# A fifth raw weight buffer, fewer early conditioning products and a later gate in a two-layer decoder trunk

## The chip, the cores and the metric

The kernel runs on one core of one Trainium2 chip. The metric is the device time of one execution in microseconds (us). The core has TensorE for matrix products (PE in the profile, its weight loads PEld), VectorE (DVE), ScalarE (ACT), GpSimd (POOL) and SyncE (SP), whose queue starts nearly all DMA transfers here. Lower is better.

## The reference

Two layers of a decoder trunk, 256 tokens by 1024 features, in float32. Each layer has three sublayers: a SwiGLU feed-forward block (FFN), a token mixer, and a second FFN. Layer 0 mixes tokens with an HGRN2 gated linear recurrence, layer 1 with a chunked gMLP. Around each sublayer stand an RMSNorm before and after, and a shift, scale and gate that come from the conditioning vector c:

```python
cond = silu(c)
mod = (cond @ ada_w[i] + ada_b[i])            # 9 vectors of 1024 per layer
h = rms_norm(x, pre_g) * (1.0 + scale) + shift
x = x + res_w * gate * rms_norm(fn(h), post_g)
# fn of an FFN: (silu(h @ w_a) * (h @ w_b)) @ w_out
# fn of HGRN2, per head, with b the running sum of log f in chunks of 64 tokens:
#   log_f = logaddexp(log lb, log1p(-lb) + log_sigmoid(fx));  k = (1 - lb) * sigmoid(-fx)
#   o = (q exp(b)) @ state + sum over s <= t of q_t exp(b_t - b_s) k_s v_s
#   state = state * exp(b_last) + sum of k exp(b_last - b) v
#   out = (rms_norm(o) * silu(g)) @ w_out
```

## The kernel before

**Products.** TensorE multiplies in a form with rounded operands (fp32r). To keep the accuracy of float32, every weight and every activation is split into a high and a low part, and each product is three: high by high, high by low, low by high (`mm3`, L162; `mm3f`, L462; `out_mm`, L416). So every weight tile is loaded in two halves of 128x1024 into a buffer of the pool `raw`, rounded by ScalarE into the high tile (`cast`, L113, the copy at L122) and subtracted by VectorE to give the low tile (`sub`, L129, at L132). High and low tiles come from the pool `whl` of 14. `raw` has 4 buffers: a load into one can start when the subtraction that read it last is done. All loads stand in SP's queue in program order (`load`, L56), so a load that waits for its buffer holds those behind it.

**Conditioning products.** The shift, scale and gate vectors are 144 products of VectorE (`ada`, L181, the product at L194), each over a 128x1024 tile of 512 KB that has to be loaded first. `pace` (L156) spreads them over the weight blocks: `pace(upto, blocks)` sets a rate, and `wblock` (L141) does so many products for each block prepared, up to a limit. The norm before the second sublayer needs the first 40 of them, that before the third needs 64. In the first sublayer the limit is 50 (`bgs["ffn0"]`), spread over 23 blocks; the boundary to the second adds two; in the HGRN sublayer the limit is 64, spread over 9 blocks.

**The order of work.** Between sublayers and in their first units (`open`, L303, to `close`, L392) the order on TensorE, VectorE and ScalarE is the written one. Elsewhere a scheduler places instructions at compile time by program order, readiness and buffers, but `after` (L59) holds one instruction behind another on its engine. `self.gate` holds a product behind another product, `self.hold` holds casts, subtractions and conditioning products behind given ones, and `table` (L72) places ScalarE's function tables between their users.

**The head** (`start`, L1107, and `first_h`, L1167). c is spread to all partitions by a product (L1125), `cond` is its silu. The sums of squares of x (L1133) give r; the two 128x1024 tiles of x are scaled by r, the first half of the features on VectorE (L1143), the second on ScalarE (L1145), transposed by TensorE (L1149) and copied by ScalarE into `xnT` (L1150), 16 transposes and 4 copies in all. Between the square root and the rest the silu table is loaded. The first products (L578) go by blocks of 128 features, `kc` 0 to 7: for each block `first_h` makes two conditioning products, from these the columns `A` and `sh` (L1173, L1174), then `hf = A * xnT + sh` on ScalarE (L1177), its rounding to the high part on ScalarE (L1179) and the low part on VectorE (L1180); 48 products follow, sorted in the first seven blocks by part. They gather in eight PSUM banks, four of which are those that held the transposes.

**The HGRN sublayer** (`hgrn`, L648). The eight heads are worked in two halves of four. For each half `feat` (L656) makes the projections of f and q in pairs of heads (`pr` 0 and 1); `gate_f` (L689) turns f's projection into k, b (the running sum) and nk: its first part (L694 to L698) reads the projection in PSUM, its second (L701 to L714) makes log f, the running sum (a scan, L710) and k. It works in a tile `L`, which for `pr` 1 is the only tile of the pool `lp`. `attn` (L716) computes the scores of a half in seven levels of halving block size: for each level `prep` (L720) makes an operand X with two subtractions and a multiplication on VectorE (L727, L732, L737) around an exponential on ScalarE, sixteen (or eight) small products follow (L755), and a masked copy (L768). `zip_steps` (L873) interleaves the levels of `attn(0)` with the projections, the gate and the values of the second half (L914 to L917), one step of the latter per level, after a lead of five; and `attn(1)` with the norm and output products of the first half (L956). `norm` (L926) scales eight 128x128 blocks of the first half's heads by their inverse norm on ScalarE (L828, called at L941); TensorE transposes them (L837), ScalarE and VectorE split them (L845, L846), and the first output products (L164) follow.

Of the kernel before, what the change touches and what calls it, by code (L numbers as in the profile page):

```python
# [10 lines left out]
F32 = mybir.dt.float32  # L11
# [4 lines left out]
ALU = mybir.AluOpType  # L16
# [17 lines left out]
class Body:  # L34
    def __init__(self, ctx, tc, ins, out):
# [4 lines left out]
        self.raw = pool("raw", 4)  # L40
# [3 lines left out]
        self.lp = pool("lp", 1)  # L44
# [444 lines left out]
    def ffn(self, f, hT, G_fn, pre_next, nxt, bg):  # L489
# [76 lines left out]
        if f == 0:  # L566
# [3 lines left out]
            for kc in range(KC):  # L570
                self.first_h(kc)
                wb = nb()
# [17 lines left out]
        if f == 0:  # L590
            self.pace(bg, 23)
        for u in range(len(pend), 11):
# [17 lines left out]
            if u == 8:  # L610
                G = G_fn()
        pre_next()
# [35 lines left out]
    def hgrn(self, hT, G_fn, pre_next, nxt, bg):  # L648
        nc, tc = self.nc, self.tc
        self.pace(bg, 9)  # L650
# [38 lines left out]
        def gate_f(hb, pr, z):  # L689

            L = self.lp.tile([P, 512], F32, tag="L", name="L") if pr else self.scr.tile([P, 512], F32, tag="hf", name="L")
# [9 lines left out]
            for h, sl in hs:  # L701
                nc.scalar.activation(L[:, sl], b[:, sl], AF.Abs, bias=col(self.ldiff, h))
            for h, sl in hs:
                nc.scalar.activation(b[:, sl], b[:, sl], AF.Relu, bias=col(self.ldiff, h))
            self.act_exp(L, L, scale=-1.0)
            self.tact(L, L, AF.Ln, bias=1.0)
            for h, sl in hs:
                nc.vector.scalar_tensor_tensor(b[:, sl], b[:, sl], col(self.loglb, h), L[:, sl],
                                               op0=ALU.add, op1=ALU.add)
                nc.vector.tensor_tensor_scan(b[:, sl], self.rmask, b[:, sl], 0.0, ALU.mult, ALU.add)  # L710
            for h, sl in hs:
                self.act_exp(k[:, sl], nk[:, sl], scale=-1.0, bias=col(self.log1mlb, h))
                nc.vector.scalar_tensor_tensor(nk[:, sl], nk[:, sl], col(self.log1mlb, h), b[:, sl],
                                               op0=ALU.subtract, op1=ALU.add)  # L714

        def attn(hb, bank, res):  # L716
# [3 lines left out]
            def prep(h):  # L720
# [7 lines left out]
                if h == 64:  # L728
                    self.act_exp(Xv[:, :, 0, :], Xv[:, :, 0, :])
                    self.act_exp(Xv[:, :, 1, :], bv[:, :, 1, :])  # L730
                else:
                    nc.vector.tensor_sub(Xv[:, :, 1, :], bv[:, :, 1, :], ref)  # L732
                    if h == 1:
                        self.act_exp(Xv[:, :, 1, :], Xv[:, :, 1, :])
                    else:
                        self.act_exp(X, X)
                return X, nc.vector.tensor_mul(Xv[:, :, 1, :], Xv[:, :, 1, :], qv[:, :, 1, :])  # L737
# [135 lines left out]
        def zip_steps(a, b, lead):  # L873

            b = list(b)
            def step():
                while b:
                    if next(b[0], a) is not a:
                        break
                    b.pop(0)  # L880
# [6 lines left out]
            self.gate = None  # L887
            run(*b)

        pg = self.res  # L890
# [35 lines left out]
        def norm():  # L926
# [13 lines left out]
            for u in range(2):  # L940
                scale(state["norm"][u], r[:, 4 * u:4 * u + 4], True)  # L941
# [165 lines left out]
    def start(self):  # L1107
# [4 lines left out]
        row = self.scr.tile([1, D + P], F32, tag="xn", name="row")  # L1112
        self.load(row[:, 0:D], self.d["c"])
# [7 lines left out]
        nc.vector.memset(row[:, D:], 1.0)  # L1121
        for h in range(2):
            hs = slice(512 * h, 512 * h + 512)
            ps = self.acc.tile([P, 512], F32, tag="acc", name="cps")
            nc.tensor.matmul(ps, row[:, D:], row[:, hs], start=True, stop=True)  # L1125
# [12 lines left out]
        self.table("silu_and_others")  # L1138
        for h in range(2):
            hs = slice(512 * h, 512 * h + 512)  # L1140
            for t in range(NT):
                if h == 0:
                    nc.vector.tensor_scalar(xn[t][:, hs], self.x[t][:, hs], r[:, t:t + 1], None, op0=ALU.mult)  # L1143
                else:
                    nc.scalar.activation(xn[t][:, hs], self.x[t][:, hs], AF.Copy, scale=r[:, t:t + 1])  # L1145
                ps = self.yps.tile([P, 512], F32, tag=f"y{t}{h}", name="xps")
                for k in range(4):
                    kc = 4 * h + k
                    nc.tensor.transpose(ps[:, k * P:(k + 1) * P], xn[t][:, kc * P:(kc + 1) * P], self.ident)  # L1149
                nc.scalar.copy(self.xnT[:, 4 * h:4 * h + 4, t * P:(t + 1) * P],  # L1150
                               ps.rearrange("p (k t) -> p k t", k=4))
# [15 lines left out]
    def first_h(self, kc):  # L1167

        nc = self.nc
        self.ada(2 * kc + 2)  # L1170
        A, sh = self.c0
# [155 lines left out]
```

## Time and profile before

Three runs took 1161.33, 1159.75 and 1160.45 us, median 1160.45. The numbers of the profile come from one more execution.

| | |
|---|---|
| profiled execution, device time | 1161.51 us |
| its span, first to last instruction | 1159.7 us |
| TensorE clock granted, mean | 0.995 |
| bytes moved by DMA | 282.31 MB, 243 GB/s in the mean |
| conditioning products, VectorE | 144, 174.8 us |
| weight subtractions (L132), VectorE | 376, 452.5 us |
| weight casts (L122), ScalarE | 376, 387.1 us |

How to read the profile: a row of a timeline gives start and duration in us, engine, line, operation, the tiles written and read, shapes and a count of merged instructions; in square brackets stands how long the engine was idle before it and what it waited for. A row of waits gives total, number and longest. A row with two times and a colon is a stretch of the span, with its length, the busy time of PE, PEld, DVE, ACT and POOL, the granted clock, the DMA share and GB/s. Spans of products overlap, since they are pipelined, so an engine's busy time is the union of its spans. Durations of a merged row are their union too.

### The profile page before, as it was taken

How to read it: one execution, taken by the hardware profiler on the slowest of the kernel's cores; microseconds unless marked ns; L12 is line 12 of the kernel's file. 1: busy time of each engine (PE TensorE's matmuls, PEld its weight loads, DVE VectorE, ACT ScalarE, POOL GpSimd, SP SyncE). 2: the span in 40 equal slices, each digit the busy share in tenths (PEclk: the TensorE clock that was granted, in tenths of full speed). 3: DMA queues.
4: the chain of work that ended last, by engine and by line, in shares of the span. 5: the costliest groups of instructions: out<-in, count | busy, mean ns of one | idle time of the engine just before them, and what ended most of it. 6: DMA issues, size and time to landing. Idle time of an engine off the chain costs nothing.

```text
span 1159.7 us, 17073 instructions
## 1 busy us (share of the span) xinstructions
PE 1133.2 (98%) x6518; PEld 987.8 (85%) x6518; DVE 897.7 (77%) x1359; ACT 672.0 (58%) x1065; POOL 6.8 (1%) x16
## 2 busy tenths in 40 slices
PE   7999999999999999999999999999999999999997
PEld 6999997799887888888888888888999888888886
DVE  6997877998797898875699986666987876775832
ACT  5453445887786764555765555644764457654631
POOL 0000000000000000000000000000000000000000
PEclk9999999999899999999999999999999999999999
DMA  9999998585434599986299987427787763875720
GB/s 345 324 329 333 330 339 317 201 305 180 145 103 147 198 351 330 341 284 202 65 356 343 331 304 252 146 84 260 258 294 259 275 219 98 266 245 195 246 100 37
DMA packets 79764, 282.31 MB, mean 243 GB/s; under 512 B 9873, under 2 KB 10561, under 8 KB 79682
## 3 DMA queue, kind: packets, MB, share of 16 engines
q1 hardware_dynamic: 78626, 278.05, 68.6%
q0 software_dynamic: 1056, 3.17, 0.7%
q8 instruction: 51, 0.84, 0.3%
q14 instruction: 31, 0.25, 0.1%
HBM read 280.11 MB, written 1.07 MB: 242 GB/s over the span
## 4 chain that ended last, share of the span: by engine, by line
PE 83%; DVE 8%; DMA 5%; ACT 2%; issue 2%; DVEq 0%; SPq 0%; ACTq 0%
PE ups L458 17%; PE ups L459 9%; PE y L164 8%; PE y L166 8%; PE y L165 8%; PE pps L433 6%; PE ups L578 4%; PE ups L464 4%; PE ups L466 4%; PE ups L465 4%; DVE w L132 3%; DMA ada<-in_ada 2%; DMA raw<-in_wffn 2%; PE ab L755 1%; DMA raw<-in_whg 1%
## 5 line engine op out<-in xcount | busy, mean ns | idle before, releaser
L132 DVE TENSOR_TENSOR w<-raw,w 128x1024 fp32r<-128x1024 f32 x376 | 452.5, 1221 | 86.0 <-ACT w L122 85.0
L122 ACT CAST w<-raw 128x1024 fp32r<-128x1024 f32 x376 | 387.1, 1049 | 150.9 <-DMA raw<-in_wffn 71.2
L458 PE MATMUL ups<-h,w 128*128 128x512 f32 x864 | 302.4, 393 | 0.1
L459 PE MATMUL ups<-h,w 128*128 128x256 f32 x864 | 242.1, 280 | 0.0
L194 DVE CUSTOM_DVE_ANT_0 ada<-ada,cond 128x1024 f32<-128x1024 f32 x144 | 174.8, 1219 | 25.9 <-DMA ada<-in_ada 25.9
L458 PEld LDWEIGHTS ups<-h,w 128*128 128x128 f32 x864 | 161.8, 187 | 37.0 <-PE ups L459 0.4
L164 PE MATMUL y<-w,t 128*128 128x512 f32 x448 | 178.1, 399 | 0.9 <-ACT t L169 0.9
L165 PE MATMUL y<-w,t 128*128 128x512 f32 x448 | 177.2, 396 | 1.4 <-DVE w L132 1.4
L166 PE MATMUL y<-w,t 128*128 128x512 f32 x448 | 176.9, 396 | 0.4 <-DVE t L170 0.4
L459 PEld LDWEIGHTS ups<-h,w 128*128 128x128 f32 x864 | 163.3, 189 | 1.0
L464 PE MATMUL ups<-h,w 128*128 128x256 f32 x416 | 118.4, 285 | 0.0
L466 PE MATMUL ups<-h,w 128*128 128x256 f32 x416 | 117.7, 283 | 0.0
L465 PE MATMUL ups<-h,w 128*128 128x256 f32 x416 | 117.6, 283 | 0.0
L433 PE MATMUL pps<-w,h 128*128 128x512 f32 x480 | 113.9, 393 | 0.7 <-DVE h L293 0.7
L433 PEld LDWEIGHTS pps<-w,h 128*128 128x128 f32 x480 | 89.0, 188 | 19.4 <-DVE h L293 1.2
L166 PEld LDWEIGHTS y<-w,t 128*128 128x128 f32 x448 | 84.2, 188 | 21.1 <-DVE t L170 1.0
L164 PEld LDWEIGHTS y<-w,t 128*128 128x128 f32 x448 | 84.3, 188 | 20.6 <-ACT t L169 1.5
L165 PEld LDWEIGHTS y<-w,t 128*128 128x128 f32 x448 | 84.3, 188 | 20.6 <-DVE w L132 2.7
L464 PEld LDWEIGHTS ups<-h,w 128*128 128x128 f32 x416 | 79.7, 192 | 1.1 <-issue 0.2
L465 PEld LDWEIGHTS ups<-h,w 128*128 128x128 f32 x416 | 79.7, 192 | 0.8 <-issue 0.2
L466 PEld LDWEIGHTS ups<-h,w 128*128 128x128 f32 x416 | 79.7, 192 | 0.0
L80 ACT ACTIVATE t<-t 128x256 f32<-128x256 f32 (+2 forms) x70 | 36.2, 522 | 39.0 <-DVE t L511 37.5
(202 smaller groups left out, 1303.7 us busy)
## 6 DMA issues: line engine op xcount, KB each, us to landing
raw<-in_wffn SPq DMA_DIRECT2D x264, 512.0 KB, 5.6
ada<-in_ada SPq DMA_DIRECT2D x144, 512.0 KB, 6.7
raw<-in_wgmu SPq DMA_DIRECT2D x48, 512.0 KB, 5.6
raw<-in_whg SPq DMA_DIRECT2D x40, 512.0 KB, 5.6
raw<-in_wgmv SPq DMA_DIRECT2D x24, 512.0 KB, 4.8
G<-gflat POOLq DMA_DIRECT2D x6, 512.0 KB, 6.5
t<-in_gbin SPq DMA_DIRECT2D x6, 256.0 KB, 5.9
x<-in_x SPq DMA_DIRECT2D x2, 512.0 KB, 4.2
```

The costliest lines, as they stand in the source:

```text
L122: self.after(self.nc.scalar.copy(hi[:, sl], raw), self.hold[0])
L132: self.after(self.nc.vector.tensor_sub(lo[:, sl], raw, hi[:, sl]), self.hold[1])
L164: self.paced(mm(ps, l[0], r[0], start=start, stop=False))
L165: mm(ps, l[0], r[1], start=False, stop=False)
L166: mm(ps, l[1], r[0], start=False, stop=stop)
L194: self.after(nc.vector.tensor_tensor_reduce(t, t, self.cond, 1.0, 0.0, ALU.mult, ALU.add, self.mod[i // 24][:, i % 24:i % 24 + 1]), self.h ...
L433: lambda g=g, i=i, j=j, kc=kc, w=w: mm(res[g][t], h2[:, i, t, kc, :], w, start=kc + i + j == 0, stop=i == 1 and kc == KC - 1)))
L458: self.paced(mm(ps, u[0], self.h2[:, :, :, kc, :], start=kc == 0, stop=False))
L459: self.last = mm(ps[:, 1, :], u[1], self.h2[:, 0, :, kc, :], start=False, stop=kc == KC - 1)
L464: self.paced(mm(o, u[0], h[0], start=start, stop=False))
L465: mm(o, u[0], h[1], start=False, stop=False)
L466: self.last = mm(o, u[1], h[0], start=False, stop=stop)
```

## The change

- **Buffers.** `raw` has five buffers. The pool `lp` is gone; the second pair's `L` in `gate_f` comes from the pool `p2` (`t2`), which has four. The row of ones for the first product moves into a tile of its own.
- **Head.** The scalings of both halves of x come first. Then only the first half of the features is transposed and copied (`turn(0)`). `first_h(0)` issues the first half weight cast ahead of its hf, rounds h with VectorE in place of ScalarE, and makes the first half weight subtraction and the other transposes and copies behind that, the copies ordered after hf. All later conditioning products and subtractions stay behind the first low part (`self.hold`). The silu table is loaded at the third block.
- **Conditioning products.** In the first sublayer up to 36 over 19 blocks, and from the ninth unit on up to 44 over 10. In the HGRN sublayer up to 64 over 11 blocks in place of 9. The total is unchanged.
- **Gate.** For the second half of the heads `gate_f` makes only its first part at once; the second (`rest`) is put into `later` and issued two steps on. Its first ScalarE operation is ordered behind the latest level's exponential, its first VectorE operation behind that level's multiplication.
- **Norm.** Of the eight scalings in `norm` the last four go to VectorE (L830's form) in place of ScalarE.

The diff, cut to its core:

```diff
-        self.raw = pool("raw", 4)
+        self.raw = pool("raw", 5)
-        self.lp = pool("lp", 1)
@@ ffn
                 self.first_h(kc)
-                wb = nb()
+                if kc == 2:
+                    self.table("silu_and_others")
+                if kc == 0:
+                    self.halves(1)
+                    wb = self.ready.pop(0)
+                else:
+                    wb = nb()
...
-            self.pace(bg, 23)
+            self.pace(36, 19)
...
                 G = G_fn()
+                if f == 0:
+                    self.pace(bg, 10)
@@ hgrn
-        self.pace(bg, 9)
+        self.pace(bg, 11)
...
-            L = self.lp.tile([P, 512], F32, tag="L", name="L") if pr else self.scr.tile([P, 512], F32, tag="hf", name="L")
+            L = self.t2() if pr else self.scr.tile([P, 512], F32, tag="hf", name="L")
...
+            def rest():
+                e, last = state.get("level", (None, None))
+                for h, sl in hs:
+                    self.after(nc.scalar.activation(L[:, sl], b[:, sl], AF.Abs, bias=col(self.ldiff, h)), e)
...
+                for h, sl in hs:
+                    self.after(nc.vector.scalar_tensor_tensor(b[:, sl], b[:, sl], col(self.loglb, h), L[:, sl],
+                                                              op0=ALU.add, op1=ALU.add), last)
+                    nc.vector.tensor_tensor_scan(b[:, sl], self.rmask, b[:, sl], 0.0, ALU.mult, ALU.add)
...
+            if hb:
+                later.extend([None, True, rest])
+            else:
+                rest()
@@ prep
-                return X, nc.vector.tensor_mul(Xv[:, :, 1, :], Xv[:, :, 1, :], qv[:, :, 1, :])
+                last = nc.vector.tensor_mul(Xv[:, :, 1, :], Xv[:, :, 1, :], qv[:, :, 1, :])
+                state["level"] = e, last
+                return X, last
@@ zip_steps
             def step():
+                if later and later.pop(0):
+                    later.pop(0)()
...
             self.gate = None
+            while later:
+                step()
             run(*b)
@@ norm
-                scale(state["norm"][u], r[:, 4 * u:4 * u + 4], True)
+                scale(state["norm"][u], r[:, 4 * u:4 * u + 4], u == 0)
@@ start
-        self.table("silu_and_others")
-        for h in range(2):
-            hs = slice(512 * h, 512 * h + 512)
+        for t in range(NT):
+            nc.vector.tensor_scalar(xn[t][:, 0:512], self.x[t][:, 0:512], r[:, t:t + 1], None, op0=ALU.mult)
+            nc.scalar.activation(xn[t][:, 512:], self.x[t][:, 512:], AF.Copy, scale=r[:, t:t + 1])
+
+        def turn(h, prev=None):
             for t in range(NT):
...
-                nc.scalar.copy(self.xnT[:, 4 * h:4 * h + 4, t * P:(t + 1) * P],
-                               ps.rearrange("p (k t) -> p k t", k=4))
+                self.after(nc.scalar.copy(self.xnT[:, 4 * h:4 * h + 4, t * P:(t + 1) * P],
+                                          ps.rearrange("p (k t) -> p k t", k=4)), prev)
+
+        turn(0)
+        self.turn = turn
@@ first_h
         self.ada(2 * kc + 2)
+        if kc == 0:
+            self.cast()
...
-        nc.scalar.activation(hf, self.xnT[:, kc, :], AF.Identity, bias=sh[:, c], scale=A[:, c])
+        full = nc.scalar.activation(hf, self.xnT[:, kc, :], AF.Identity, bias=sh[:, c], scale=A[:, c])
...
-        nc.scalar.copy(self.hT[0][:, :, kc, :], hf)
-        nc.vector.tensor_sub(self.hT[1][:, :, kc, :], hf, self.hT[0][:, :, kc, :])
+        if kc:
+            nc.scalar.copy(self.hT[0][:, :, kc, :], hf)
+        else:
+            nc.vector.tensor_copy(self.hT[0][:, :, kc, :], hf)
+        dve = nc.vector.tensor_sub(self.hT[1][:, :, kc, :], hf, self.hT[0][:, :, kc, :])
+        if kc == 0:
+            self.hold = (None, dve)
+            self.sub()
+            self.turn(1, full)
@@ run
-        bgs = {"ffn0": 50, "hg": 64, "ffn1": 92, "ffn2": 120, "gm": 138, "ffn3": 144}
+        bgs = {"ffn0": 44, "hg": 64, "ffn1": 92, "ffn2": 120, "gm": 138, "ffn3": 144}
```

More of the change, by code (lines that the diff above doesn't have):

```diff
@@ L700, in gate_f @@
             col = lambda a, h: a[:, h:h + 1]
[L701 to L714, printed above, removed]
+            def rest():
[3 more added lines that the diff above has]
+                for h, sl in hs:
+                    nc.scalar.activation(b[:, sl], b[:, sl], AF.Relu, bias=col(self.ldiff, h))
+                self.act_exp(L, L, scale=-1.0)
+                self.tact(L, L, AF.Ln, bias=1.0)
+                for h, sl in hs:
+                    self.after(nc.vector.scalar_tensor_tensor(b[:, sl], b[:, sl], col(self.loglb, h), L[:, sl],
+                                                              op0=ALU.add, op1=ALU.add), last)
+                    nc.vector.tensor_tensor_scan(b[:, sl], self.rmask, b[:, sl], 0.0, ALU.mult, ALU.add)
+                for h, sl in hs:
+                    self.act_exp(k[:, sl], nk[:, sl], scale=-1.0, bias=col(self.log1mlb, h))
+                    nc.vector.scalar_tensor_tensor(nk[:, sl], nk[:, sl], col(self.log1mlb, h), b[:, sl],
+                                                   op0=ALU.subtract, op1=ALU.add)
+            if hb:
+                later.extend([None, True, rest])
+            else:
+                rest()
         def attn(hb, bank, res):
@@ L729, in prep @@
                     self.act_exp(Xv[:, :, 0, :], Xv[:, :, 0, :])
-                    self.act_exp(Xv[:, :, 1, :], bv[:, :, 1, :])
+                    e = self.act_exp(Xv[:, :, 1, :], bv[:, :, 1, :])
                 else:
@@ L887, in zip_steps @@
             self.gate = None
+            while later:
+                step()
             run(*b)
+        later = []
         pg = self.res
@@ L1111, in start @@
         self.table("silu_and_others")
-        row = self.scr.tile([1, D + P], F32, tag="xn", name="row")
-        self.load(row[:, 0:D], self.d["c"])
+        row = self.scr.tile([1, D], F32, tag="xn", name="row")
+        one = self.scr.tile([1, P], F32, tag="hf", name="one")
+        self.load(row, self.d["c"])
         self.x = [self.const.tile([P, D], F32, name=f"x{t}") for t in range(NT)]
@@ L1120, in start @@
         self.npre = self._load("npre", [P, 6, KC])
-        nc.vector.memset(row[:, D:], 1.0)
+        nc.vector.memset(one, 1.0)
         for h in range(2):
@@ L1124, in start @@
             ps = self.acc.tile([P, 512], F32, tag="acc", name="cps")
-            nc.tensor.matmul(ps, row[:, D:], row[:, hs], start=True, stop=True)
+            nc.tensor.matmul(ps, one, row[:, hs], start=True, stop=True)
             self.tact(self.cond[:, hs], ps, AF.Silu)
@@ L1137, in start @@
         nc.vector.reciprocal(r, v)
-        self.table("silu_and_others")
-        for h in range(2):
-            hs = slice(512 * h, 512 * h + 512)
+        for t in range(NT):
+            nc.vector.tensor_scalar(xn[t][:, 0:512], self.x[t][:, 0:512], r[:, t:t + 1], None, op0=ALU.mult)
+            nc.scalar.activation(xn[t][:, 512:], self.x[t][:, 512:], AF.Copy, scale=r[:, t:t + 1])
+        def turn(h, prev=None):
             for t in range(NT):
[L1142 to L1145, printed above, removed]
                 ps = self.yps.tile([P, 512], F32, tag=f"y{t}{h}", name="xps")
```

4 lines of the change are left out of this document (2 added, 2 removed).

## The prediction

> **What bounds the kernel now.** I read the page's busy times first, then busy time by stage, then TensorE's own waits, then the timeline at each of those waits. Busy times and chain, from the page:
>
> ```profile
> span 1159.7 us, 17073 instructions
> PE 1133.2 (98%) x6518; PEld 987.8 (85%) x6518; DVE 897.7 (77%) x1359; ACT 672.0 (58%) x1065; POOL 6.8 (1%) x16
> PE 83%; DVE 8%; DMA 5%; ACT 2%; issue 2%; DVEq 0%; SPq 0%; ACTq 0%
> ```
>
> TensorE is busy 1133.2 of 1159.7 us, and the change leaves no product out, so what can be won is the idle 26.5 us, plus time at a reduced clock. The stage table (us from the start: stretch length, then busy time of each engine, granted clock, DMA share) says where it lies:
>
> ```profile
> 0.00:15.94 15.94, 7.42 (x21) 4.43 (x21) 6.79 (x17) 10.50 (x16) 0.20 (x4) 1.00 0.88 318
> 15.94:64.00 48.06, 48.06 (x388) 48.06 (x389) 44.16 (x72) 26.54 (x37) 0.00 (x0) 1.00 0.91 324
> 64.00:186.00 122.00, 122.00 (x851) 113.77 (x851) 99.06 (x139) 53.58 (x61) 1.21 (x2) 1.00 0.94 340
> 186.00:240.00 54.00, 51.00 (x251) 41.45 (x250) 47.21 (x79) 41.64 (x74) 0.00 (x0) 1.00 0.73 253
> 240.00:360.00 120.00, 114.18 (x806) 105.57 (x805) 101.64 (x160) 88.15 (x149) 1.07 (x2) 0.97 0.48 168
> ```
>
> The head is idle 8.5 us; the first sublayer proper (64 to 186) loses nothing, but its DMA share is 0.94; its end (186 to 240) is idle 3.0, the HGRN stage 5.8, and there alone the clock is below 1. TensorE's waits name what comes late (total, times, longest):
>
> ```profile
> PE xps L1149 <- DVE xn L1143: 3.6, 1, 3.6
> PE ab L755 <- DVE t L737: 3.1, 3, 1.6
> PE ups L578 <- ACT h L1179: 2.4, 1, 2.4
> PE y L165 <- DVE w L132: 1.4, 3, 0.6
> PE y L164 <- ACT w L845: 1.2, 1, 1.2
> ```
>
> The first of these waits for the statistics of x, which the change doesn't touch. The other four are what it aims at.
>
> **The change, part by part.**
>
> *Head.* The timeline before the first product (start, duration, engine, line):
>
> ```profile
> 9.09 1.28 ACT L74 ACT_TABLE_LOAD   x1
> 10.39 0.73 ACT L1145 ACTIVATE xn<-x,r 128x512 f32<-128x512 f32 x1
> 11.63 1.67 ACT L1150 COPY w<-xps 128x512 f32<-128x512 f32 x3
> 12.71 0.22 DVE L1174 SCALAR_TENSOR_TENSOR A<-mod,ab,npre 128x1 f32<-128x1 f32 x1
> 14.05 0.60 ACT L1177 ACTIVATE hf<-w,shift,A 128x256 f32<-128x256 f32 x1
> 14.55 1.03 ACT L122 CAST w<-raw 128x1024 fp32r<-128x1024 f32 x1
> 15.48 0.40 ACT L1179 CAST h<-hf 128x256 fp32r<-128x256 f32 x1
> 15.61 1.23 DVE L132 TENSOR_TENSOR w<-raw,w 128x1024 fp32r<-128x1024 f32 x1 [2.69 <-ACT w L122]
> 15.94 44.31 PE L578 MATMUL ups<-h,w 128*128 128x256 f32 x355 [2.41 <-ACT h L1179]
> 20.63 0.22 DVE L1174 SCALAR_TENSOR_TENSOR A<-mod,ab,npre 128x1 f32<-128x1 f32 x1
> ```
>
> Until 14 us ScalarE is one queue: table load, two scalings, four copies, then hf, a weight cast and the cast of h. The change moves the load behind the second step and two copies behind hf, and gives the cast of h to VectorE. hf can then start when its column A is there, 12.71 + 0.22, about 13.0, or 0.5 later if the first weight cast (1.03) runs ahead of it. Then 0.6 for hf and the copy on VectorE, a form the trace lacks: between nothing and the 0.43 of a subtraction of that shape on the same engine (L1180, below); I take 0.4. The first product starts near 14.4, 1.5 us earlier. But the next steps hang on VectorE, which is busy 44.16 of 48.06 us there. Behind h's low half at about 14.4 it has that subtraction (0.43), two weight halves and two conditioning products (four of about 1.2: rows L132 and L194) before the second column A, so about 19.7 against 20.63 + 0.22 in the trace. So **-1.1**, between 0 and the -1.5 of the start. The moved table load (1.28) falls where ScalarE has 21.5 us idle of 48 (second row of the stage table); without that cover it costs 1.28.
>
> ```profile
> L1180 DVE TENSOR_TENSOR h<-hf,h 128x256 fp32r<-128x256 f32 x8 | 3.4, 425 | 0.2
> L194 DVE CUSTOM_DVE_ANT_0 ada<-ada,cond 128x1024 f32<-128x1024 f32 x144 | 174.8, 1219 | 25.9 <-DMA ada<-in_ada 25.9
> SPq L57 <- DVE w L132: 673.0, 289, 16.6
> ```
>
> *44 instead of 50 products before the first boundary.* Six products leave the first sublayer with their DMAs: 6 x 512 KB, 3.1 MB, at the stage's 340 GB/s 9 us of transfers in a stretch whose DMA share is 0.94. TensorE's three waits for weights (L165 on L132, 1.4 us) come at its end, this one the last and longest:
>
> ```profile
> 194.81 0.50 PE L165 MATMUL y<-w,t 128*128 128x512 f32 x1 [0.65 <-DVE w L132]
> ```
>
> 9 us more lead, less the 1.1 that TensorE starts earlier, covers them: **-1.4**, between 0 and that. What is late next is the boundary's own chain of statistics, which stays.
>
> The six go into the HGRN sublayer, at 1219 ns each 7.3 us of VectorE, with six DMA issues in SP's queue. There:
>
> ```profile
> 230.00:310.00 80.00, 76.99 (x566) 73.30 (x565) 70.21 (x116) 62.30 (x102) 0.52 (x1) 0.96 0.59 208
> ```
>
> VectorE has 9.8 us free of 80. 7.3 fits by the sum, but only where its idle time can be filled; behind a product stand the weight halves and the level preparations that TensorE waits for. Bounds 0 and **+7.3**; nearer to 0, as 9.8 is over 7.3; I take **+1.5**.
>
> *Gate two steps later.* Around the longest level wait:
>
> ```profile
> 285.05 1.89 PE L755 MATMUL ab<-t 128*128 128x64 f32 x16
> 287.86 0.87 DVE L708 SCALAR_TENSOR_TENSOR w<-w,loglb,L 128x256 f32<-128x256 f32 x2
> 288.65 1.26 DVE L710 TENSOR_TENSOR_SCAN w<-rmask,w 128x256 f32<-128x256 f32 x2
> 289.84 0.85 DVE L713 SCALAR_TENSOR_TENSOR w<-w,log1mlb 128x256 f32<-128x256 f32 x2
> 290.61 0.68 DVE L737 TENSOR_TENSOR t<-t,w 128x512 f32<-128x512 f32 x1
> 291.43 2.81 PE L755 MATMUL ab<-t 128*128 128x64 f32 x16 [1.58 <-DVE t L737]
> 292.00:300.00 8.00, 8.00 (x33) 6.87 (x32) 6.21 (x9) 4.95 (x10) 0.00 (x0) 0.57 0.21 66
> ```
>
> The gate's second half (L708, L710, L713) holds VectorE for 2.8 us directly ahead of the multiplication that TensorE waits for. Put two steps later, and ordered behind each level's last operations, it lets L737 go up to 2.8 earlier: **-1.6**. The gate's results are needed only by the second half's attention, which starts two steps or more after it.
>
> Right behind this wait the clock drops: 0.57 over 8 us, which is 3.4 us of lost work (the same sixteen products take 2.81 instead of 1.89). If the wait goes, that spell may go: between 0 and -3.4. TensorE would then catch up with VectorE and with the raw tiles, so I count **-2.0**.
>
> By the Trainium skill (TensorE: Matmul & The Clock Gate, section "Part 1: The HAM clock gate") the clock falls only after a whole idle window of about 3.4 us; here it fell after a gap of 1.58 us, so the trace speaks against that rule. By the rule this term would be 0.
>
> *Head outputs.* The second group of four scalings goes from ScalarE to VectorE:
>
> ```profile
> 336.79 2.45 ACT L828 ACTIVATE t<-t,r 128x128 f32<-128x128 f32 x8
> 340.81 0.50 PE L164 MATMUL y<-w 128*128 128x512 f32 x1 [1.19 <-ACT w L845]
> L830 DVE TENSOR_SCALAR t<-t,r x4: 280/281/286, 356.3 to 356.9; 128x128 f32<-128x128 f32 x4
> ```
>
> Half of the 2.45 us, 1.2, leaves the chain to L845, and VectorE does the other four in 0.9 beside it: **-1.0**, between 0 and the wait's 1.2.
>
> *Fifth raw buffer, lp gone.* SP waits 673 us for subtractions (L132) that free a raw tile; that is the queue that all loads stand in. One more tile moves each raw load up by one tile. It shows where a load ends a chain on TensorE:
>
> ```profile
> 317.38 1.04 ACT L122 CAST w<-raw 128x1024 fp32r<-128x1024 f32 x1 [5.07 <-DMA raw<-in_whg]
> 326.07 1.97 PE L755 MATMUL ab<-t 128*128 128x64 f32 x16 [1.19 <-DVE t L737]
> ```
>
> Of that 1.19 I take **-0.6**, between 0 and -1.2. L of the second pair now shares the t2 buffers: no cost seen, as it lives two steps only.
>
> **Sum**: -1.1 - 1.4 + 1.5 - 1.6 - 2.0 - 1.0 - 0.6 = -6.2. The profiled execution took 1161.51 us (span 1159.7 and 1.8 around it), so 1155.3 for it; it lies 1.06 above the median of 1160.45, from which the same sum gives **1154.2**.
>
> **Rivals.**
> 1. *VectorE becomes the bound of HGRN* (slower). None of its 9.8 us can be filled, since they stand behind loads and TensorE's own results; the 7.3 us land on TensorE and eat the level gains, with only head and weights won: +7.3 - 2.5 gives 1165.2. It decides as soon as more than 2.5 of the 7.3 reach TensorE and nothing else is won. For it: 88% busy there, and products that waited for their loads. Against: the same loads come earlier with a fifth tile.
> 2. *Same*: all that I count is won, but the products cost their bound: -6.2 - 1.5 + 7.3 = -0.4, 1160.0.
> 3. *Only head and weights pay*; in HGRN one wait follows another: -2.5, 1158.0.
> 4. *The clock drops all the same*, elsewhere or for another reason: -6.2 + 2.0, 1156.2. For it: it fell once in a stretch of several short waits, and not all of these go. The Trainium skill's rule above (TensorE: Matmul & The Clock Gate) would have it so.
> 5. *Everything is won*, products hidden: the head's 1.5, the weights' 1.4, all 5.8 idle of the HGRN stage and the clock's 3.4, together -12.1: 1148.4.
> That the change doesn't do what it says, that is, the first product still waits behind ScalarE, takes away 1.1: 1155.3, inside the forecast.
>
> **How the numbers follow.** Forecast 0.50 (about 1150 to 1157); rival 4 0.13, rival 3 0.13, rival 2 0.10, rival 1 0.09, rival 5 0.05. A measurement tells about 0.2%, 2.3 us, from no change, so faster means under 1158.1: 0.50 + 0.13 + 0.05 and half of rival 3, 0.75; same 0.16; slower 0.09. The range runs from a little below rival 5, 1148.0, to 1161.5, past rival 2; it leaves out rival 1.
>
> **What would show it.** Head: L578's first start near 14.4 and its last end about 1 us earlier. Weights: no wait of L165 on L132 before 200 us. Gate: L708 to L713 of the second half of the heads behind the levels' L737, no 1.58 wait, clock 1.00 from 292 to 300. Outputs: L845's wait under 0.5. Wrong would be VectorE above 76 us busy in 230 to 310 with more waits of TensorE for L737 or L132 there.

## The result and the profile after

| | median | range | runs |
|---|---|---|---|
| before | 1160.89 us | 1159.50 to 1162.52 | 6 |
| after | 1153.87 us | 1152.55 to 1155.14 | 6 |

The ratio is 0.9937, 95% interval 0.9924 to 0.9949: 7.0 us less. The profiled execution took 1153.41 us at a mean clock of 0.995. From the page of the kernel after: span, busy times, the chain that ended last, and two rows of the costliest groups (busy time, mean ns | idle time before them and what ended most of it):

```profile
span 1151.6 us, 17120 instructions
PE 1130.6 (98%) x6518; PEld 987.8 (86%) x6518; DVE 898.2 (78%) x1364; ACT 668.0 (58%) x1060; POOL 6.8 (1%) x16
...
PE 90%; DVE 6%; ACT 1%; DMA 1%; issue 1%; DVEq 0%; ACTq 0%
...
L131 DVE TENSOR_TENSOR w<-raw,w 128x1024 fp32r<-128x1024 f32 x376 | 451.5, 1219 | 78.0 <-ACT w L121 72.4
L121 ACT CAST w<-raw 128x1024 fp32r<-128x1024 f32 x376 | 384.1, 1048 | 139.7 <-DMA raw<-in_wffn 45.8
```

TensorE's idle time is 21.0 us where it was 26.5 (span less busy). The two profiled spans differ by 8.1 us: 5.5 of it is this idle time, 2.6 is busy time (1133.2 to 1130.6, with the same 6518 products), of which no run shows the cause. Line numbers have shifted: the weight cast was L122 and is L121, the subtraction L132 is L131, the score products L755 are L773, the level multiplication L737 is L753. The page of before shows for the cast:

```profile
L122 ACT CAST w<-raw 128x1024 fp32r<-128x1024 f32 x376 | 387.1, 1049 | 150.9 <-DMA raw<-in_wffn 71.2
```

Casts waited 71.2 us for their loads and now wait 45.8. The stage table of after, cut at the same events as before's (first product; the same 48.06 and 122.00 us; the same distance behind the first HGRN projection and behind the last score product), and the fixed stretch 230 to 310:

```profile
0.00:14.54 14.54, 7.42 (x21) 4.43 (x21) 7.20 (x19) 8.06 (x12) 0.20 (x4) 1.00 0.87 307
...
62.60:184.60 122.00, 122.00 (x850) 113.62 (x849) 98.14 (x132) 55.54 (x64) 1.21 (x2) 1.00 0.90 326
184.60:235.20 50.60, 50.00 (x251) 41.83 (x250) 42.08 (x72) 37.65 (x70) 0.00 (x0) 1.00 0.64 225
235.20:353.45 118.25, 113.51 (x806) 105.16 (x805) 108.64 (x177) 87.67 (x146) 1.07 (x2) 0.97 0.56 202
230.00:310.00 80.00, 78.15 (x604) 74.58 (x603) 76.81 (x124) 62.36 (x104) 1.07 (x2) 1.00 0.67 242
```

Against before the head is 1.40 us shorter (15.94 to 14.54), the end of the first sublayer 3.4 (54.00 to 50.60), the HGRN stage 1.75 (120.00 to 118.25), and 1.5 more is gained behind it: the last product starts 8.06 us earlier. The waits of TensorE in after, the six longest totals:

```profile
PE xps L1171 <- DVE xn L1163: 3.6, 1, 3.6
PE cps L1149 <- DMA row<-in_c: 2.4, 1, 2.4
PE tps L163 <- DVE t L765: 2.1, 1, 2.1
PE ab L773 <- DVE t L753: 1.3, 2, 0.9
PE ups L583 <- ACT w L121: 1.1, 1, 1.1
PE tps L535 <- DVE t L530: 0.9, 1, 0.9
```

Of the four that the prediction aimed at, the waits for weights and for the norm's output are gone, the first product's wait (L583) is 1.1 (was 2.4) and the level wait 1.3 (was 3.1). One is new: L163 waiting for L765, the masking of the first score products of the second half of the heads, which frees their PSUM bank. The timeline of after at that wait:

```profile
310.84 1.05 ACT L121 CAST w<-raw 128x1024 fp32r<-128x1024 f32 x1 [1.94 <-DMA raw<-in_whg]
...
313.55 1.22 DVE L131 TENSOR_TENSOR w<-raw,w 128x1024 fp32r<-128x1024 f32 x1 [0.41 <-ACT w L121]
...
314.69 1.28 DVE L765 TENSOR_TENSOR t<-ab,ident 128x512 f32<-128x512 f32 x2
...
315.52 0.77 PE L163 MATMUL tps<-w,h 128*128 128x512 f32 x1 [2.06 <-DVE t L765]
```

And the stretch behind it, in the view by windows:

```profile
316.00:320.00 4.00, 4.00 (x11) 3.08 (x10) 3.86 (x7) 4.00 (x11) 0.00 (x0) 0.50 0.67 265
```

L765 stands in VectorE's queue behind weight subtractions, these behind casts, and the casts behind loads. After the 2.06 us gap TensorE runs at half clock, as it did after the 1.58 us gap at 290 in before. So the spell that the prediction hoped to lose has moved from 292 to 315.

### The profile page after: what moved, and what is told of

The parts are those of the page before. It is cut to its first block, busy times and chain, and to the rows that moved or that the text cites. A ratio compares the mean times of both kernels' runs of the same rounds, so it can differ in the third digit from the quotient of the medians.

```text
span 1151.6 us, 17120 instructions
## 1 busy us (share of the span) xinstructions
PE 1130.6 (98%) x6518; PEld 987.8 (86%) x6518; DVE 898.2 (78%) x1364; ACT 668.0 (58%) x1060; POOL 6.8 (1%) x16
## 4 chain that ended last, share of the span: by engine, by line
PE 90%; DVE 6%; ACT 1%; DMA 1%; issue 1%; DVEq 0%; ACTq 0%
PE ups L457 17%; PE y L163 9%; PE y L164 9%; PE y L165 9%; PE ups L458 9%; PE pps L432 8%; PE ups L465 4%; PE ups L463 4%; PE ups L464 4%; PE ups L583 4%; DVE w L131 2%; PE pps L164 1%; PE pps L163 1%; PE pps L165 1%; PE ab L773 1%; PE fps L464 1%
## 5 line engine op out<-in xcount | busy, mean ns | idle before, releaser
L131 DVE TENSOR_TENSOR w<-raw,w 128x1024 fp32r<-128x1024 f32 x376 | 451.5, 1219 | 78.0 <-ACT w L121 72.4
L121 ACT CAST w<-raw 128x1024 fp32r<-128x1024 f32 x376 | 384.1, 1048 | 139.7 <-DMA raw<-in_wffn 45.8
L193 DVE CUSTOM_DVE_ANT_0 ada<-ada,cond 128x1024 f32<-128x1024 f32 x144 | 174.4, 1218 | 18.9 <-DMA ada<-in_ada 18.8
L163 PE MATMUL y<-w,t 128*128 128x512 f32 x448 | 178.4, 399 | 0.0
L165 PEld LDWEIGHTS y<-w,t 128*128 128x128 f32 x448 | 84.2, 188 | 20.3
L163 PEld LDWEIGHTS y<-w,t 128*128 128x128 f32 x448 | 84.3, 188 | 19.2
L79 ACT ACTIVATE t<-t 128x256 f32<-128x256 f32 (+2 forms) x78 | 41.0, 533 | 35.0 <-DVE t L510 32.7
```

What stands on the lines that cost most here:

```text
L121: self.after(self.nc.scalar.copy(hi[:, sl], raw), self.hold[0])
L131: self.after(self.nc.vector.tensor_sub(lo[:, sl], raw, hi[:, sl]), self.hold[1])
L163: self.paced(mm(ps, l[0], r[0], start=start, stop=False))
L165: mm(ps, l[1], r[0], start=False, stop=stop)
L193: self.after(nc.vector.tensor_tensor_reduce(t, t, self.cond, 1.0, 0.0, ALU.mult, ALU.add, self.mod[i // 24][:, i % 24:i % 24 + 1]), self.h ...
```

## The experiments

Two theories stood against each other: that of the prediction's sum, in which each edit is worth the wait that it removes and the fifth buffer least (0.6 us); and that of the buffer as the main part, with the rest deciding where the gaps lie. Twelve kernels were run, all with repeated timing: parts taken out of the changed kernel, and parts put into the kernel before.

| kernel | median us | ratio to before (95%) | mean clock | profiled us | lost at low clock |
|---|---|---|---|---|---|
| before | 1160.89 | 1 | 0.995 | 1161.51 | 3.4 |
| after | 1153.87 | 0.9937 (0.9924 to 0.9949) | 0.996 | 1153.41 | 3.4 |
| u_raw | 1158.97 | 0.9985 (0.9968 to 1.0001) | 0.995 | 1160.60 | 3.4 |
| u_raw_pace | 1157.33 | 0.9975 (0.9961 to 0.9988) | 0.997 | 1157.45 | 1.7 |
| u_head | 1156.64 | 0.9965 (0.9948 to 0.9982) | 0.995 | 1157.92 | 4.9 |
| u_gate | 1155.40 | 0.9957 (0.9944 to 0.9970) | 0.997 | 1154.46 | 1.7 |
| u_scale | 1155.46 | 0.9950 (0.9934 to 0.9966) | 0.997 | 1155.13 | 3.4 |
| u_pace | 1152.07 | 0.9934 (0.9912 to 0.9955) | 0.998 | 1152.36 | 1.7 |
| u_gate_pace | 1154.13 | 0.9943 (0.9923 to 0.9963) | 0.997 | 1154.04 | 1.7 |
| p_raw | 1159.43 | 0.9996 (0.9984 to 1.0009) | 0.993 | 1161.66 | 6.8 |
| p_head | 1159.74 | 0.9999 (0.9987 to 1.0011) | 0.996 | 1155.18 | 0 |
| p_raw_head | 1157.11 | 0.9974 (0.9959 to 0.9990) | 0.995 | 1155.86 | 3.4 |
| lead0 | 1154.35 | 0.9954 (0.9940 to 0.9969) | 0.997 | 1153.95 | 1.7 |
| u_pace_lead0 | 1154.11 | 0.9947 (0.9928 to 0.9965) | 0.996 | 1155.25 | 5.0 |

The row of before is the comparison of the section above; its clock is that of the runs beside the first experiments. Names with u_ are the changed kernel without a part, with p_ the kernel before plus a part. The mean clock is that of all timed runs. The last column is worked out from the profiled execution: the span was cut into stretches of 4 us, and for every stretch with a granted clock below 0.95 one minus the clock was multiplied by 4. In stretches of 1 us u_head and u_pace_lead0 each come to 5.1. Ratios compare with runs of before on the same chip.

**One part undone: the buffer.**

```diff
-        self.raw = pool("raw", 5)
+        self.raw = pool("raw", 4)
```

> All of the change with four raw buffers. My theory (the fifth is worth little, it only moves a load up by one tile): no wait for weights before 200 us, HGRN 0 to 1.2 us later, later sublayers the same; ratio to before 0.9935 to 0.995. Rival (the fifth buffer took the waits at the end of the first sublayer and those of 949 us away): waits of 1.4 us for a weight subtraction come back between 185 and 200 us, and 1 us or more between 930 and 960 us: ratio 0.996 to 0.9975.

1158.97 us: 5.1 more than after, nearly the whole gain, and above both expected ranges. Of the waits that the rival named, those near 950 us come back, those before 200 us don't. The cast's row on the page of u_raw:

```profile
L121 ACT CAST w<-raw 128x1024 fp32r<-128x1024 f32 x376 | 387.1, 1049 | 150.5 <-DMA raw<-in_wffn 73.0
```

Its timeline in HGRN, and one row of a late sublayer:

```profile
316.68 1.05 ACT L121 CAST w<-raw 128x1024 fp32r<-128x1024 f32 x1 [2.18 <-DMA raw<-in_whg]
...
317.76 1.23 DVE L131 TENSOR_TENSOR w<-raw,w 128x1024 fp32r<-128x1024 f32 x1 [1.41 <-ACT w L121]
...
318.90 0.68 DVE L765 TENSOR_TENSOR t<-ab,ident 128x512 f32<-128x512 f32 x1
...
323.34 2.71 PE L773 MATMUL ab<-t 128*128 128x64 f32 x16 [3.91 <-DVE A L208]
...
949.89 0.50 PE L163 MATMUL y<-w,t 128*128 128x512 f32 x1 [0.74 <-ACT t L168]
```

The casts' wait for loads is back at 73.0 us. Load, cast, subtraction, L765 in VectorE's order: the chain that costs after 2.06 us ends here in 3.91 (the row names A L208, but that is a small operation that VectorE did last; the level's operand, L753, was done at 323.2). Small waits in late sublayers come back as well, such as the one at 949.89; in before a like one of 0.86 stands at 951, and after has none there. The first boundary is untouched: it is reached 4.85 us earlier than in before, with four buffers as with five (4.73). What four buffers cost comes from HGRN on.

**The head undone.** `start` and `first_h` as before, no early silu table change.

> All of the change with the head as before (silu table, all transposes and copies ahead of the first product, h rounded by ScalarE). My theory: first product at 15.9 in place of 14.5 us, and the 1.4 us stay to the end: ratio to before 0.9945 to 0.9955. Rival (the sublayer is bound by its transfers, so the head's lead is used up): the first boundary starts within 0.5 us of the changed kernel's, ratio 0.993 to 0.994.

1156.64 us, 2.8 more than after, where its own start is 1.4 later (first product again at 15.94). The theory's mechanism holds, its price is too small: in the profiles u_head is 1.5 us behind after at the first boundary, 2.5 near 300 us, 2.9 at the last score product and 4.5 at the end. These are the waits of u_head that are longer than in after (0.9 and 2.1 there, and none of the third kind over 0.3):

```profile
PE tps L535 <- DVE t L530: 2.6, 2, 1.7
...
PE tps L163 <- DVE t L759: 2.4, 1, 2.4
...
PE ab L799 <- ACT t L79: 1.0, 1, 1.0
```

**The gate undone.**

```diff
-            if hb:
-                later.extend([None, True, rest])
-            else:
-                rest()
+            rest()
```

> All of the change but the gate's second half, which is issued at once again. My theory (the gate's second half holds VectorE ahead of the level's multiplication): a wait of TensorE of about 1.6 us for that multiplication comes back between 270 and 295 us, the time is 1.6 to 3.6 us above the changed kernel (ratio to before 0.995 to 0.997), and the half-clock spell follows that wait again. Rival (HGRN lost elsewhere what the gate won): the last score product of HGRN ends within 0.7 us of the changed kernel's, ratio 0.993 to 0.9945.

1155.40 us, 1.5 more; the intervals overlap a little. The edit takes back the two steps only. The order behind the latest level's last operations stays, so in u_gate the gate can't come ahead of that level's multiplication as it does in before. Two rows of the waits of u_gate, and its timeline at the first of them:

```profile
PE tps L164 <- DVE w L131: 2.2, 1, 2.2
PE ab L770 <- DVE t L750: 1.9, 2, 1.6
```

```profile
295.01 0.86 DVE L724 SCALAR_TENSOR_TENSOR w<-w,log1mlb 128x256 f32<-128x256 f32 x2
...
295.78 1.22 DVE L131 TENSOR_TENSOR w<-raw,w 128x1024 fp32r<-128x1024 f32 x1
...
297.06 0.50 PE L164 MATMUL tps<-w,h 128*128 128x512 f32 x1 [2.22 <-DVE w L131]
```

Issued at once, the gate's second half (its last operation is L724) stands directly ahead of a weight subtraction, and TensorE waits 2.22 us for that. This is the mechanism of the prediction, on another operand. The wait of 1.6 us for the level's multiplication comes back as well, with a spell of half clock behind it, but at 319 us and not between 270 and 295. The old wait's place, first in before (the level's exponentials), then in after:

```profile
287.32 1.99 ACT L80 ACTIVATE t<-t 128x1024 f32<-128x1024 f32 x2
```

```profile
292.41 1.05 ACT L79 ACTIVATE t<-t 128x1024 f32<-128x1024 f32 x1
...
292.51 1.22 DVE L193 CUSTOM_DVE_ANT_0 ada<-ada,cond 128x1024 f32<-128x1024 f32 x1
...
293.66 0.69 DVE L753 TENSOR_TENSOR t<-t,w 128x512 f32<-128x512 f32 x1
...
294.50 1.97 PE L773 MATMUL ab<-t 128*128 128x64 f32 x16 [0.94 <-DVE t L753]
```

The gate's operations did leave that place, and 0.94 of the 1.58 us remains. In after a conditioning product (L193, 1.22 us) stands directly ahead of the level's multiplication (L753), but it can hold it for 0.2 us at most: L753 also needs its level's exponential on ScalarE, which ended at 293.46, 0.20 us before L753 began. In before the exponentials were done by 289.31, 1.3 us or more ahead of the multiplication at 290.61, and VectorE's gate operations held it. So the wait has passed from VectorE to the level's own chain through ScalarE. In the profiles the last score product of HGRN comes 0.65 us earlier without the delay than with it (7.21 us ahead of before against 6.56); the 1.5 us are lost later. So the delay pays at most 1.5 us, and not at the wait it was aimed at.

**The paces undone.**

```diff
-            self.pace(36, 19)
+            self.pace(bg, 23)
...
-                if f == 0:
-                    self.pace(bg, 10)
...
-        self.pace(bg, 11)
+        self.pace(bg, 9)
...
-        bgs = {"ffn0": 44, "hg": 64, "ffn1": 92, "ffn2": 120, "gm": 138, "ffn3": 144}
+        bgs = {"ffn0": 50, "hg": 64, "ffn1": 92, "ffn2": 120, "gm": 138, "ffn3": 144}
```

> All of the change but the conditioning products: 50 over 23 blocks, then 64 over 9, as before. My theory (the six products' transfers make the last raw tiles of the first sublayer late): TensorE's waits for a weight subtraction between 185 and 200 us come back, about 1.4 us of waits or more, and the first transposes of the first boundary start 1.9 to 3.3 us later than in the changed kernel; HGRN wins 0 to 2 back; ratio to before 0.994 to 0.996. Rival (the fifth raw buffer took those waits away): no such wait comes back, the first boundary starts within 0.7 us of the changed kernel's, HGRN gains up to 2, ratio 0.991 to 0.9935.

1152.07 us, the lowest median of all, but its interval (0.9912 to 0.9955) covers that of after: no difference is shown. Weights are waited for at 190 us again, as this row of its waits shows (before had 1.4):

```profile
PE y L164 <- DVE w L131: 0.9, 3, 0.6
```

The first boundary is 1.4 us later than in after, and HGRN gives all of that back: its last score product is 2.4 us earlier than in after. So the theory's mechanism is there, smaller than expected, and the ratio is in the rival's range. Moving the products has a gain and a price, and they cancel within what these runs can tell.

**The norm undone.**

```diff
-                scale(state["norm"][u], r[:, 4 * u:4 * u + 4], u == 0)
+                scale(state["norm"][u], r[:, 4 * u:4 * u + 4], True)
```

> The changed kernel with all eight scalings of the norm on ScalarE as before. Theory 'the norm's wait was worth its 1.0 us': the wait for L863 near 335 us is about 1.2 us again and the time is 1154.7 to 1155.5 us. Rival 'it is hidden': the output products find the wait already covered by what ends later, L863's wait is below 0.6 or is given back by 400 us, and the time is within 0.5 us of the changed kernel's 1153.9 us.

1155.46 us, 1.6 more than after, again with overlapping intervals. The time fits the first theory, the mechanism doesn't: no wait for L863 came back. What is longer among the waits of u_scale is the one for L765 at 313 us (2.1 in after), which stands ahead of the norm:

```profile
PE tps L163 <- DVE t L765: 3.6, 1, 3.6
```

So this run settles nothing about the norm.

**One part alone.** Five buffers put into the kernel before (without `lp`, the ones in a tile of their own):

> The kernel before with the fifth raw buffer alone (and lp gone, as that makes room). Theory A (the buffer moves loads up wherever SP stood behind a subtraction, whatever the products do): the waits for weights between 185 and 200 us and those of 945 to 955 us go, HGRN shortens by 2 or more: ratio to before 0.994 to 0.9965. Theory B (it only pays for the 18 conditioning products that the change puts into HGRN; with 12 there, four buffers are enough): HGRN from the first transposes of the first boundary to its last score product is within 0.8 us of before, ratio 0.9965 to 0.999.

The new head put into the kernel before:

> The kernel before with the new head alone. My theory (the head's lead is 1.4 us and is carried through): first product at 14.4 to 14.6, ratio to before 0.9985 to 0.999. Rival A (the sublayer is bound by its transfers with four buffers, so the waits for weights at its end grow by the lead): first boundary within 0.5 us of before, ratio 0.9995 to 1.0005. Rival B (undoing the head cost 3 us, so it is worth 3 alone too): ratio 0.997 to 0.998.

1159.43 and 1159.74 us: neither differs from before, although undoing them costs 5.1 and 2.8. By the times alone no theory that gives each part a fixed price holds both. With the buffer the waits for weights near 190 us shrink (1.4 to 0.9), those near 950 go, and HGRN is 1.1 us longer in the profile: neither theory has that. The head's ratio is rival A's, but not by its mechanism: the profiled first boundary is 1.5 us earlier than in before. The casts' row and two waits of p_raw:

```profile
L121 ACT CAST w<-raw 128x1024 fp32r<-128x1024 f32 x376 | 383.6, 1048 | 146.9 <-DMA raw<-in_wffn 50.9
...
PE ab L745 <- ACT grow L222: 3.1, 1, 3.1
...
PE y L163 <- ACT w L844: 1.2, 1, 1.2
```

The casts' wait for loads falls by 20.3 us (71.2 to 50.9) without a gain in time. The stretches at the two waits, by windows:

```profile
300.00:308.00 8.00, 5.68 (x22) 5.33 (x23) 4.73 (x7) 7.08 (x10) 1.07 (x2) 0.60 0.28 100
338.00:346.00 8.00, 7.94 (x33) 7.17 (x33) 6.25 (x9) 7.94 (x10) 0.00 (x0) 0.57 0.20 67
```

TensorE falls to half clock twice, once at each of these waits, and loses 6.8 us where before loses 3.4. The 1.19 us wait of the norm's output is there in before too, but there no spell followed it. The timed runs agree in kind: p_raw ran at a mean clock of 0.9932, the runs of before beside it at 0.9953. Mean time by mean clock, 1159.4 x 0.9932 = 1151.5 against 1160.1 x 0.9953 = 1154.7, is 3.2 us lower with the buffer. That is an estimate, and a bound: it takes all time to go with the clock, and in the runs of before less than half of that is seen (last section). The same estimate gives 2.5 us for the buffer undone (u_raw 1158.6 x 0.9945 = 1152.2, after 1154.0 x 0.9963 = 1149.7). So a part of the difference between its worth alone and its worth undone may be the clock; how much, these runs don't tell.

For the head the reverse happened: its profiled execution kept the full clock up to its last product and took 1155.18 us, while its nine other runs took 1157.7 to 1161.5 us at 0.994 to 0.996. Time by clock is 1154.6 against 1154.7. So in those nine runs the 1.5 us of the head are lost somewhere that no trace shows.

**Two and three parts.** Buffer and head in the kernel before:

> The kernel before with two parts of the change together: five raw buffers and the new head; pace, gate and norm as before. Each part alone gave nothing (1159.43 and 1159.74 us), yet each cost 3 to 5 us when it was taken out of the changed kernel. Theory 'they need each other': a head start of TensorE is only kept if the weights keep up with it, and weights that come earlier only help a TensorE that isn't held up elsewhere; then the two together give most of the gain, 1153.5 to 1156.5 us, ratio 0.994 to 0.997. Theory 'the gate and the norm are needed': the level waits of HGRN take back what the two win, and the time is 1158 to 1160 us, ratio above 0.998, with a wait of the score products of 2 us or more near 300 us.

The same with the norm's scalings (the changed kernel without gate and paces):

> The changed kernel with the gate's rest at once and the paces 50/23 and 64/9 as before: what is left of the change is the buffer, the head and the norm scalings. Undone one at a time the gate cost 1.5 us and the pace gave 1.8. Theory 'buffer, head and norm are the change': 1153 to 1156 us, and lower than the kernel with buffer and head alone by at most 1.2 us, the norm's wait. Theory 'the gate's delay is what makes room for the old pace': HGRN stalls on the level operands again and the time is above 1157 us.

1157.11 and 1154.13 us. Together the two parts give 0.9974, which neither gave alone, and with the norm 0.9943, as much as the whole change within its interval. The stretch of 8 us at the norm's wait, by windows, of p_raw_head:

```profile
335.00:343.00 8.00, 8.00 (x45) 7.31 (x46) 6.70 (x10) 7.94 (x9) 0.00 (x0) 0.79 0.22 73
```

And of u_gate_pace:

```profile
333.00:341.00 8.00, 7.63 (x50) 6.90 (x51) 7.79 (x10) 7.94 (x10) 0.00 (x0) 1.00 0.23 67
```

With eight scalings on ScalarE the wait is 1.19 us and the clock falls behind it (0.79 over 8 us, 1.7 us lost); with four it is 0.78 us and the clock stays. Together that is 2.1 us; the profiled executions differ by 1.8 (1155.86 and 1154.04). In p_raw_head's timing the two theories meet halfway: the parts do need each other, and more is needed. That this is the norm is likely, not shown: u_gate_pace, like u_gate, also keeps the order of the gate's second half behind the latest level, which p_raw_head has not. Up to the 3.1 us wait near 300 us, which both have, the two are within 0.4 us of each other, so the delay of the gate is not needed. u_gate_pace is as fast as after. It lies 3.0 us under p_raw_head, where 1.2 was allowed: I had not counted a spell at the norm's wait. Such a spell isn't certain either, since before and p_head have the same 1.19 us wait without one.

**Buffer by pace.**

> The changed kernel with four raw buffers and the old paces (50/23, 64/9), so 12 products in HGRN in place of 18. Theory 'the fifth buffer pays for the six products moved into HGRN': without them four buffers are enough, and the time is 1154 to 1156 us. Theory 'the fifth buffer pays for itself, whatever the pace': as with four buffers and the new pace, 1158 to 1160 us, with the stall of the score products behind a subtraction near 319 us there again.

1157.33 us. With the old paces the fifth buffer is worth 5.3 us (1157.33 less 1152.07; 4.8 by the ratios), with the new ones 5.1: it pays whatever the pace. The time lies between the two ranges, nearer to the second, and the stall near 319 us that the second theory names is there, the longest of three waits for levels (319 to 321.7):

```profile
PE ab L771 <- DVE t L751: 5.1, 3, 3.0
...
321.71 1.97 PE L771 MATMUL ab<-t 128*128 128x64 f32 x16 [3.02 <-DVE t L751]
```

**Away with the new wait.** The lead of `attn(1)` set to 0, which puts L765 ahead of six subtractions:

```diff
-            tok(lambda t, ps: nc.scalar.copy(gg[:, t, 512:], ps), norm), outs()], 1)
+            tok(lambda t, ps: nc.scalar.copy(gg[:, t, 512:], ps), norm), outs()], 0)
```

> The changed kernel with one thing more: the second half's attention is issued one step earlier against the token projection (lead 0 in place of 1), so that on VectorE the masking of its first products stands ahead of six weight subtractions in place of behind them. My theory (what is left in HGRN is VectorE's order: that masking stands behind subtractions which wait for late raw tiles): the wait of 2.1 us near 313 us goes and the half-clock spell behind it too, ratio to before 0.989 to 0.992. Rival (raw tiles are late anyway, the wait moves to a weight): TensorE waits 1.5 us or more for a subtraction or a level between 300 and 325 us, ratio 0.993 to 0.995.

The same with the old paces:

> The same lead 0, with the conditioning products as before (50, then 64 over 9 blocks). If the products in HGRN cost VectorE time there (my theory), this is 1 to 3 us faster than lead 0 with the new pace: ratio 0.987 to 0.991. If the new pace pays at the first boundary as much as it costs in HGRN (rival), both are within 0.8 us of each other.

1154.35 and 1154.11 us, no difference, so the second rival holds. In lead0 the wait at 313 us went, and the last score product came 2.9 us earlier than in after, partly because lead 0 puts it earlier in the order; but another gap took the wait's place, with its own drop of the clock (1.7 us). From the timeline of lead0, and from its waits (L535 had 0.9, once, in after):

```profile
330.96 2.71 PE L773 MATMUL ab<-t 128*128 128x64 f32 x16 [2.37 <-DVE t L753]
...
PE tps L535 <- DVE t L530: 2.4, 2, 1.4
```

At the second boundary 1.5 us of the lead is left, and the wait of 1.4 for L530 at 395 us, which after doesn't have, takes that. The theory that the wait at 313 us is what is left to win falls. The rival holds in kind, since the wait moves, but to 331 us in place of 300 to 325, and its ratio (0.9954) is just above the rival's range. No version beat the changed kernel by more than its interval.

## Why the prediction was right, and where it was not

The forecast was 1154.2 us and the time 1153.87: right in sum (7.0 us won, 6.2 to 6.7 forecast from either base), but the terms did not fall as put down. That the sum came out is in part luck: two terms failed, one was far too small, and the errors had opposite signs.

- **Head, -1.1 (0 to -1.5):** right. First product 14.54 (14.4 forecast), the copy on VectorE 0.29 us inside its bounds of 0 and 0.43, the second column A at 19.20 and 0.22 (19.7 forecast), the last L578 product 1.45 earlier; the stretch behind lost nothing to the moved table load. Undone, it cost 2.8 us; put into before, it gave nothing that the times show.
- **Weights, -1.4:** right, and too small. No wait for L131 is left before 200 us. That stretch is 3.4 us shorter; among the rest is this wait in the timeline of before, which I had counted with the chain of statistics that stays. It is gone in after, in u_raw and in p_raw, and is there in u_raw_pace (1.4 us), so either the new pace or the fifth buffer takes it away:

```profile
207.06 0.66 PE L271 MATMUL npa<-ident,xn 128*128 128x128 f32 x4 [1.02 <-DVE be L244]
```

- **Six products in HGRN, +1.5 (0 to +7.3):** the balance was right: weights and products together were put at +0.1, and undoing both made no difference that the intervals show. VectorE is busy 76.81 us of 230 to 310, above the 76 that I had named as a warning, but the level waits fell from 3.1 to 1.3 us. (After is some 5 us ahead there, so the same stretch holds later work.) Rivals 1 and 2 did not come.
- **Gate, -1.6:** the order changed as said (L719 to L724 now run at 297 to 300, behind the level's L753), but only 0.6 of the 1.58 us came. The step that failed is that L737 could go 2.8 us earlier once VectorE is free: I did not ask when its other operand would be ready. The level's exponential on ScalarE ended 0.20 us before the multiplication began; the moved product that stands in the free place adds 0.2 at most.
- **Clock, -2.0 (0 to -3.4):** failed in the profile. The spell moved and cost the same 3.4 us. Rival 4, that the clock drops elsewhere, is what happened; its time was missed since other terms were larger. The expected clock of 1.00 from 292 to 300 is there, the spell only stands 20 us later.
- **Norm, -1.0:** not settled. No wait for L863 is left in after, but u_scale, with all eight scalings on ScalarE, has none either, and its 1.6 us more stand with a longer wait for L765. For the term speak p_raw_head and u_gate_pace, where that wait goes from 1.19 to 0.78.
- **Fifth buffer, -0.6 (0 to -1.2):** mis-sized, by the times the largest error. I priced one load wait of 1.19 us on TensorE. The runs give 5.1 us when it is undone, at a clock that is lower too (2.5 if all time went with the clock). The row that should have set its upper bound was the casts' 71.2 us of waiting for loads, which fell by 25.4. It is a bound and no price: in p_raw they fell by 20.3 and the time stayed. In u_raw one can follow how such a wait reaches TensorE: late load, cast, subtraction, and behind it in VectorE's queue L765 and the level's operand.

So by this account what the buffer and the weights gave beyond their terms covered what clock and gate did not bring. It is an account and no sum: undone one at a time, buffer, head, gate and norm cost 11.0 us and the paces give 1.8 back, 9.2 together, where the change wins 7.0. Three points stay open: why the head alone is worth nothing in most of its runs, what the norm is worth apart from the clock spell at its wait, and how much of the buffer's 5.1 us is the clock.

## What to carry to other kernels

Bound the worth of a further load buffer by the wait of the first consumer for its loads over the whole kernel, not by the one place where a load shows on TensorE. When an operation is moved out of the way of a critical one, write down when each of that one's other operands is ready, on every engine. Where the clock falls after short waits, a part tried alone may show nothing because it has only shifted a gap: compare the granted clock beside the time before judging it, and take parts out of the full change as well as putting them in.

## What the hardware showed

- In the fourteen profiles, up to the last product, the low clock (0.50) came in spells that cost 1.7 or 3.4 us and once 5.1 (u_pace_lead0), which is 3.4, 6.8 and 10.2 us at half speed. One stands in the head (u_head, 17 to 20 us), all others between 290 and 348 us. Each began at a wait of TensorE: in after, u_scale, u_head and p_raw (its first) while it was still idle, in the others within 2.5 us behind the wait.
- The wait at which a spell began was 1.19 us (p_raw's second, p_raw_head's second), 1.4 to 1.7 (u_raw's first, u_gate, before, u_pace), 2.1 to 2.4 (after, lead0, u_pace_lead0, u_head twice), 3.0 to 3.1 (u_raw_pace, p_raw, p_raw_head, u_gate_pace), 3.62 (u_scale) and 3.91 us (u_raw's second). The Trainium skill (TensorE: Matmul & The Clock Gate, Part 1) has a full idle window of about 3.4 us as the condition; only the last two are as long. The length alone doesn't decide either: the wait of 3.6 us for x in the head brought no fall in any profile, and p_head kept the full clock over this wait, a twin of the one at 291 in before (its timeline, then the HGRN stage by windows):

```profile
287.93 1.97 PE L761 MATMUL ab<-t 128*128 128x64 f32 x16 [1.57 <-DVE t L743]
```

```profile
240.00:360.00 120.00, 114.05 (x814) 104.87 (x813) 102.46 (x162) 91.04 (x154) 1.07 (x2) 1.00 0.46 160
```

- A spell isn't always time lost. In u_head the one at 17 us cost 1.7 us by the clock, but its last L577 product ended at 63.78 us, that of before, without a spell and with the same start, at 63.73.
- The runs of before beside the experiments, by their mean clock: 1158.9 us in the mean of six at 0.999, 1161.0 in the mean of eighteen at 0.995. The difference is 2.1 us, where time that went wholly with the clock would give 4.6. Over all 63 of these runs the clock accounts for about a quarter of the variance of the time.
